# A hybrid decoder layer on one core: the split of the next stage's third weight chunk tied behind the first token block's squares and gain products

## The chip, the cores and the metric

The kernel runs on one core of one Trainium2 chip. The metric is the device time of one execution in microseconds (us), and a kernel's time is the median of its runs. The engines are TensorE (PE in the profile, its weight loads PEld), VectorE (DVE), ScalarE (ACT), GpSimd (POOL) and SyncE (SP, which here only issues loads).

## The reference

One decoder layer over 256 tokens of width 1024 in float32: a SwiGLU block, a mixer (a Mamba-2 branch and a differential attention branch, merged by gates), and a second SwiGLU block. Each stage has a norm in front and one behind:

```python
h = h + 0.5 * rmsnorm(swiglu(rmsnorm(h, ffn1_pre_g[l]), ffn1_w_gate[l], ffn1_w_up[l], ffn1_w_down[l]),
                      ffn1_post_g[l])
u = rmsnorm(h, mix_pre_g[l])
z, xbc, dt_raw, q, k, v, gate_logits = jnp.split(u @ w_in[l], IN_SPLITS, axis=-1)
...
h = h + rmsnorm(merged @ w_out[l], mix_post_g[l])
h = h + 0.5 * rmsnorm(swiglu(rmsnorm(h, ffn2_pre_g[l]), ffn2_w_gate[l], ffn2_w_up[l], ffn2_w_down[l]),
                      ffn2_post_g[l])
```

So there are two turns from one stage to the next: the first SwiGLU into the mixer, and the mixer into the second SwiGLU. At each, a product's result goes through the norm behind the old stage, is added to h, goes through the norm in front of the new stage, and is multiplied by the new stage's first weights.

## The kernel before

**Weights.** All weights are read once, in chunks of 1 MB that are listed in the order of their use. `load_to` issues the load of a chunk on SP into one of three `raw` buffers. A matmul takes a float32 number as two parts: `split_steps` makes, for each half of a chunk, a rounded part `whi` by a cast on ScalarE (L250) and the rest `wlo = raw - whi` by a subtraction on VectorE (L253). Each product is then three matmuls, hi by hi, lo by hi and hi by lo. When all four instructions of a chunk are done its raw buffer is free, and the load of the chunk three further on goes into it. `split_to(n)` splits the chunks up to the n-th, `ahead_of(i, n)` says which chunk lies n ahead of the i-th, and `take` hands out a chunk's parts, splitting some way ahead (`AHEAD` is 3).

**The turn.** The tokens are two blocks of 128. `mm_n` is the last product of a stage, with weights of its own. It keeps the last three chunks (`TAIL`) back and multiplies block 0 with all of them first, its 512-wide left half and then its right half, so that block 0's norm can run while TensorE does block 1. In `mm_n`, `ready(0)` puts block 0's norm into the program, `split_to(ahead_of(taken[0], AHEAD - 1))` the split of the next stage's first two chunks, then come block 1's matmuls (with `turned()` between its halves, which transposes block 0's new h and puts its gain in), `split_to(ahead_of(taken[0], AHEAD))` with the third chunk, and `ready(1)`, block 1's norm.

**The norm behind a stage**, `post_norm`, handles a half at a time. `sum_sq` squares it on ScalarE and sums along the row (L442, `jp_f` or `jp_mxp`). VectorE multiplies the half by the gain (L541, `og`). Behind `mm_quads` the half is first summed from two parts on VectorE (L785: `p_f` and `u_f` for block 0's halves, `u_f` and `c_f` for block 1's). POOL makes the reciprocal root, an add and a power (L447, L448, `rp`), and VectorE updates h (L550). The norm in front of the next stage squares h on ScalarE (`sq_mx`, `sq_f`), and POOL makes `r_mx` or `r_f`. For block 0, the class `Norm` transposes h itself on TensorE (L456, `pu_mx`, `pu_f`) and ScalarE and VectorE make the hi and lo parts with the gain (L462, L464, `u_mx`, `u_f`), the row factor coming later. For block 1, VectorE first multiplies by the factor (L501, `un_mx`, `un_f`), and TensorE transposes that. `products` is the next stage's first products, `pn_mx` and `pn_f` (L335): 12 matmuls for each of four chunks and each block, block 0 first, with block 1's transposes written after the third twelve.

**What sets the order.** From `own_order(PE)` in `mm_n` to the end of `products`, TensorE's instructions run as they are written, and a scheduler that works with estimated times places those of the other engines. An instruction waits for what it reads, and each engine runs its own queue in order.

Of the kernel before, what the change touches and what calls it, by code (L numbers as in the profile page):

```python
# [16 lines left out]
F32 = mybir.dt.float32  # L17
F32R = mybir.dt.float32r
AF = mybir.ActivationFunctionType
ALU = mybir.AluOpType  # L20
# [8 lines left out]
D = 1024  # L29
# [24 lines left out]
def tile_hybrid_layer(ctx: ExitStack, tc: tile.TileContext, x, ffn1_pre_g, ffn1_w_gate, ffn1_w_up,  # L54
# [4 lines left out]
    nc = tc.nc  # L59
# [5 lines left out]
    def k4(shape, name, dt=F32):  # L65
        return sb.tile(shape, dt, tag="k4", name=name, bufs=K4_BUFS)
# [4 lines left out]
    def k2(shape, name, dt=F32):  # L71
        return sb.tile(shape, dt, tag="k2", name=name, bufs=K2_BUFS)

    def jk(shape, name):
        return sb.tile(shape, F32, tag="jk", name=name, bufs=2)

    def tiny(n, name):
        return sb.tile([P, n], F32, tag=f"tiny{n}", name=name, bufs=10)
# [5 lines left out]
    def pjt(name):  # L84

        return pj(name).rearrange("p (m t) -> p m t", m=2)

    def bg(shape, name):
        return ps.tile(shape, F32, tag="bg", name=name, bufs=5)
# [127 lines left out]
    ffn_chunks("f2", ffn2_w_gate, ffn2_w_up, ffn2_w_down)  # L217

    raws, splits = [], []
    taken = [0]  # L220

    def load_to(n):
        while len(raws) < min(n, len(chunks)):
            i = len(raws)
            src, shape = chunks[i]
            r = sb.tile(shape, F32, tag="raw", name=f"raw{i}", bufs=RAW_BUFS)
            nj = shape[1] // 4 if i == 0 else shape[1] // 2 if i < 4 else shape[1]
            for j in range(0, shape[1], nj):
                nc.sync.dma_start(r[:, j:j + nj, :], src[:, j:j + nj, :])
            raws.append(r)  # L230

    def split_steps(ahead=True):


        i, _ = units[len(splits)]
        load_to(i + 1)
        r, shape = raws[i], chunks[i][1]
        nj = shape[1] // 2
        his, los = [], []
        splits.append((his, los))  # L240
        for q in range(2):
            hi = k4([P, nj, shape[2]], f"whi{i}{q}", F32R)
            lo = k4([P, nj, shape[2]], f"wlo{i}{q}", F32R)
            his.append(hi)
            los.append(lo)
            n = 1 if i == 0 else nj
            for j in range(0, nj, n):
                js = slice(j, j + n)
                copy = nc.scalar.copy if i + q + j else nc.vector.tensor_copy
                copy(hi[:, js, :], r[:, q * nj + j:q * nj + j + n, :])  # L250
                if not i + q + j:
                    yield
                nc.vector.tensor_sub(lo[:, js, :], r[:, q * nj + j:q * nj + j + n, :], hi[:, js, :].bitcast(F32))  # L253
                yield
        raws[i] = None
        if ahead:
            load_to(i + 1 + RAW_BUFS)

    def split_to(n):

        while len(splits) < min(n, len(units)):
            of, p = units[len(splits)]
            if p is not None:
                splits.append(of.split(p))
                continue
            for _ in split_steps():
                pass

    def ahead_of(i, n):

        n *= 4
        while n > 0 and i < len(units):
            n -= 4 if units[i][1] is None else 1
            i += 1
        return i

    def take(ahead=AHEAD):

        i = taken[0]
        taken[0] += 1  # L280
        split_to(ahead_of(i, ahead))
        (of, p), w = units[i], splits[i]
        splits[i] = None
        if p is not None:
            return w
        his, los = w
        nj = chunks[of][1][1] // 2
        return (lambda j: his[j // nj][:, j % nj, :], lambda j: los[j // nj][:, j % nj, :])
# [63 lines left out]
    order = mybir.DependencyInfo(mybir.DependencyClass.NoSync, mybir.DependencyReason.DATA)  # L352
# [8 lines left out]
    def act(*args, **kw):  # L361
        a = nc.scalar.activation(*args, **kw)
        if act_fence[0] is not None:
            tc.add_manual_dep(a.ins, act_fence[0], order, reason="activation table")
        act_since.append(a.ins.name)
# [4 lines left out]
    def own_order(*engines):  # L370

        if not ordered[0]:
            order_of[0].enter_context(tc.manual_schedule(engines=set(engines)))
            ordered[0] = True
# [13 lines left out]
    halves = (slice(0, 512), slice(512, D))  # L388
# [32 lines left out]
    for name, v in (("mx", mix_pre_g), ("f2", ffn2_pre_g),  # L421
                    ("ng", ssd_norm_g), ("cb", ssd_conv_b), ("sg", da_subln_g)):
        n = v.shape[1] // P
# [15 lines left out]
    def sum_sq(ss, src, fold, name):  # L439

        junk = jk([P, 512], name)
        nc.scalar.activation(junk, src, AF.Square, scale=(fold / D) ** 0.5, accum_out=ss)  # L442

    def rstd_of(ss, fold, name):

        r = tiny(1, name)
        nc.gpsimd.tensor_scalar(r, ss[:, 0:1], ss[:, 1:2], fold * EPS, ALU.add, ALU.add)  # L447
        f = nc.gpsimd.tensor_tensor(r, r, nhalf, ALU.pow)  # L448
        last_pool[0] = f.ins
        return r  # L450
# [80 lines left out]
    def post_norm(b, acc, pg, fold, tag, last=False):  # L531

        ss = tiny(2, f"sp_{tag}{b}")
        og = []
        for q in range(2):
            sum_sq(ss[:, q:q + 1], acc[q], fold, f"jp_{tag}{b}{q}")
            if last and q == 0:
                e = tiny(1, f"ep_{tag}{b}")
                nc.vector.tensor_scalar(e, ss[:, 0:1], fold * EPS, None, ALU.add)
            og.append(k2([P, 512], f"og_{tag}{b}{q}"))  # L540
            nc.vector.tensor_tensor(og[q], acc[q], pg[:, halves[q]], ALU.mult)  # L541
        if last:
            r = tiny(1, f"rp_{tag}{b}")
            act(r, ss[:, 1:2], AF.Ln, bias=e)
            act(r, r, AF.Exp, scale=-0.5)
        else:
            r = rstd_of(ss, fold, f"rp_{tag}{b}")
        for q in range(2):
            hq = h[:, b, halves[q]]
            nc.vector.scalar_tensor_tensor(hq, og[q], r, hq, ALU.mult, ALU.add)  # L550

    def load_gain(v, name):
        pg = k4([P, D], name)
        nc.gpsimd.dma_start(pg, v[0].partition_broadcast(P))
        return pg

    def mm_n(acc, acts, ready, turned, begun=lambda: None, pairs=None, begin=True, taken_all=lambda: None):

        pairs = pairs or range(len(acts) // 2)
        n = len(pairs)
        held = []

        def one(i, w, parts):
            wh, wl = w
            for kt in range(2):
                ah, al = acts[2 * pairs[i] + kt]
                for b, qs in parts:
                    ts = slice(b * P, (b + 1) * P)  # L570
                    for x_, w_ in ((ah, wh), (al, wh), (ah, wl)):
                        for q in qs:
                            nc.tensor.matmul(acc[b][q], x_[:, ts], w_(kt)[:, halves[q]],  # L573
                                             start=begin and i == 0 and kt == 0 and x_ is ah and w_ is wh,
                                             stop=i == n - 1 and kt == 1 and w_ is wl)
                if i == 0:
                    begun()

        for i in range(n):
            w = take(min(n - i, AHEAD))  # L580
            if i < n - TAIL:
                one(i, w, ((0, (0, 1)), (1, (0, 1))))
            else:
                held.append((i, w))
        taken_all()
        own_order(PE)
        for q in range(2):
            for i, w in held:
                one(i, w, ((0, (q,)),))
        ready(0)  # L590
        split_to(ahead_of(taken[0], AHEAD - 1))
        for q in range(2):
            for i, w in held:
                if q == 1 and i == n - TAIL:
                    turned()
                one(i, w, ((1, (q,)),))
        split_to(ahead_of(taken[0], AHEAD))
        ready(1)

    def sums_of(g, even, odd):  # L600
# [130 lines left out]
    def ffn(post_v, tag, ready, turned, then, products):  # L731
# [51 lines left out]
        def done(b):  # L783
            for q in range(2):
                nc.vector.tensor_tensor(rest[b][q], acc[b][q], rest[b][q], ALU.add)  # L785
            post_norm(b, rest[b], pg, 4.0, tag, ready is store)
            ready(b)

        mm_n(acc, gu, done, turned, pairs=pairs, begin=False,
             taken_all=combine)  # L790

# [16 lines left out]
    raised(1, 0)  # L808
    warm(FILL)
    steps = split_steps(False)  # L810
    next(steps)
    raw(0, 0)
# [75 lines left out]
    norm = made[0]  # L888
# [142 lines left out]
    for i in range(4):  # L1031
        acc = pjt(f"pbc{i}")
# [284 lines left out]
    for g in range(4):  # L1317
        xs[g] = k4([P, 4, T], f"xs{g}")
        for i in range(2):
            acc = pjt(f"pxs{g}{i}")  # L1320
# [5 lines left out]
    for g in range(4):  # L1326
        sz[g] = k4([P, 4, T], f"sz{g}")
        for i in range(2):
            acc = pjt(f"pz{g}{i}")
# [98 lines left out]
    pg = load_gain(mix_post_g, "pg_mx")  # L1428
    acc = [[bg([P, 512], f"acc_mx{b}{q}") for q in range(2)] for b in range(2)]
# [3 lines left out]
    def mixed(b):  # L1433
        post_norm(b, acc[b], pg, 1.0, "mxp")
        ready(b)

    mm_n(acc, mg, mixed, turned, lambda: turn_merged(1))


    norm = made[0]  # L1440
# [36 lines left out]
```

## Time and profile before

| what | value |
|---|---|
| median of 3 runs | 737.97 us (737.88 to 738.38) |
| the profiled execution's own time | 737.54 us |
| span of its records | 735.8 us |
| loads from HBM | 136.17 MB, 187 GB/s over the span |
| the cast L250, 225 of them | 1044 ns mean |
| the subtraction L253, 226 of them | 1208 ns mean |

A row of the timeline is: start in us from the span's start, length in us, engine, line, operation, output and inputs, shapes, count, and in brackets the engine's idle time before it and what ended it. Rows of the same kind are merged, with their count. Instructions of one engine overlap a little, so a step is better read from start to start than from a length. In a view of stretches each row has the stretch, its length, the busy time of TensorE, its weight loads, VectorE, ScalarE and POOL with the number of instructions, the granted TensorE clock as a share of full speed, the busy share of the DMA engines, and GB/s.

### The profile page before, as it was taken

Reading aid. Unit: us, or ns where it says so; the run is one execution under the profiler, and the core shown is the slowest. Engines: PE = TensorE matmul, PEld = TensorE weight load, DVE = VectorE, ACT = ScalarE, POOL = GpSimd, SP = SyncE. Lnnn points to the kernel's source line nnn. Section 1 sums busy time; section 2 is a strip of 40 time slices with the busy share of each in tenths; the row PEclk is TensorE's granted clock in tenths of the full one; section 3 lists DMA queues with packets and bytes.
Section 4 is the critical chain, followed back from the end, with each engine's and each line's share of the span. In section 5 each row is a group of like instructions: output and inputs, shape, how many; then the busy total and the mean of one; then the engine's idle time right before and its main releaser. Section 6 shows DMA issues by size and latency. Waiting matters only on the chain.

```text
span 735.8 us, 10869 instructions
## 1 busy us (share of the span) xinstructions
PE 726.4 (99%) x4211; PEld 628.1 (85%) x4211; DVE 591.9 (80%) x904; ACT 462.1 (63%) x777; POOL 38.6 (5%) x72
## 2 busy tenths in 40 slices
PE   8999999999999999999999999999999999999996
PEld 6888888888889999999888788888888888888874
DVE  7978768998677878787996998785784878779994
ACT  7657556665566565958975577782663657566562
POOL 2700000000300000000000000000010000000000
PEclk9999999999999999999999999999999999999998
DMA  8884674469353647567464664475470765664541
GB/s 299 229 261 150 218 229 171 155 216 348 118 172 117 201 143 226 192 188 226 146 219 154 202 222 138 152 238 191 127 241 34 229 199 153 222 217 143 188 168 57
DMA packets 94212, 137.96 MB, mean 187 GB/s; under 512 B 2684, under 2 KB 68304, under 8 KB 94160
## 3 DMA queue, kind: packets, MB, share of 16 engines
q1 hardware_dynamic: 91488, 129.51, 54.2%
q0 software_dynamic: 2368, 7.22, 3.1%
q8 instruction: 33, 0.54, 0.3%
q10 hardware_dynamic: 304, 0.53, 0.2%
q14 instruction: 19, 0.16, 0.1%
HBM read 136.17 MB, written 1.08 MB: 187 GB/s over the span
## 4 chain that ended last, share of the span: by engine, by line
PE 97%; DVE 2%; issue 1%; DMA 0%; ACT 0%; DVEq 0%
PE pup_f L316 9%; PE pg_f L316 9%; PE pgt L335 6%; PE pws L335 6%; PE acc_f1p L625 5%; PE acc_f2p L625 4%; PE pg_f L315 4%; PE pup_f L315 4%; PE pn_f L335 3%; PE pn_mx L335 3%; PE acc_mx L573 3%; PE pn_f L345 3%; PE pwd L335 3%; PE acc_f1p L573 3%; PE pz L302 2%; PE pxs L304 2%
## 5 line engine op out<-in xcount | busy, mean ns | idle before, releaser
L253 DVE TENSOR_TENSOR wlo<-raw,whi 128x1024 fp32r<-128x1024 f32 (+1 forms) x226 | 266.6, 1208 | 22.7 <-ACT whi L250 21.7
L250 ACT CAST whi<-raw 128x1024 fp32r<-128x1024 f32 (+1 forms) x225 | 226.2, 1044 | 18.1 <-DMA raw<-in_w_in_dram 3.8
L316 PE MATMUL pup_f<-u_f,whi 128*128 128x512 f32 x288 | 101.3, 396 | 0.0
L316 PE MATMUL pg_f<-u_f,whi 128*128 128x512 f32 x288 | 101.2, 396 | 0.0
L315 PE MATMUL pg_f<-u_f,wlo 128*128 128x256 f32 x252 | 70.6, 280 | 0.0
L315 PE MATMUL pup_f<-u_f,wlo 128*128 128x256 f32 x252 | 70.3, 279 | 0.0
L316 PEld LDWEIGHTS pup_f<-u_f,whi 128*128 128x128 f32 x288 | 52.8, 188 | 9.8
L316 PEld LDWEIGHTS pg_f<-u_f,whi 128*128 128x128 f32 x288 | 52.8, 188 | 9.6
L315 PEld LDWEIGHTS pg_f<-u_f,wlo 128*128 128x128 f32 x252 | 47.5, 188 | 1.7
L315 PEld LDWEIGHTS pup_f<-u_f,wlo 128*128 128x128 f32 x252 | 47.5, 189 | 1.6
L321 DVE TENSOR_TENSOR su_f<-pup_f,su_f 128x256 f32<-128x256 f32 x36 | 15.1, 420 | 26.0 <-ACT su_f L320 25.8
L130 ACT CAST wqh<-wt 128x1024 fp32r<-128x1024 f32 x20 | 21.0, 1052 | 23.2 <-DVE wt L122 23.2
L320 ACT COPY su_f<-pup_f 128x256 f32<-128x256 f32 x36 | 13.4, 373 | 35.1 <-PE pup_f L316 34.9
L335 PE MATMUL pgt<-whi,u_mx 128*128 128x512 f32 x128 | 33.1, 393 | 0.0
L301 PE MATMUL pxs<-u_mx,whi 128*128 128x256 f32 x128 | 31.7, 285 | 0.0
L302 PE MATMUL pz<-u_mx,whi 128*128 128x256 f32 x128 | 31.6, 284 | 0.0
L301 PE MATMUL pz<-u_mx,whi 128*128 128x256 f32 x128 | 31.6, 284 | 0.0
L302 PE MATMUL pxs<-u_mx,whi 128*128 128x256 f32 x128 | 31.4, 283 | 0.0
L335 PEld LDWEIGHTS pgt<-whi,u_mx 128*128 128x128 f32 x128 | 23.6, 188 | 5.4 <-issue 0.7
L1009 DVE SCALAR_TENSOR_TENSOR xs<-pxs,cols_b,xs 128x255 f32<-128x255 f32 (+2 forms) x48 | 21.9, 475 | 6.3 <-ACT xs L1006 5.9
L291 ACT CAST gh_f<-sg_f 128x512 fp32r<-128x512 f32 x18 | 11.2, 622 | 21.5 <-DVE sg_f L771 21.5
L302 PEld LDWEIGHTS pz<-u_mx,whi 128*128 128x128 f32 x128 | 24.5, 192 | 0.2 <-issue 0.2
(397 smaller groups left out, 1698.5 us busy)
## 6 DMA issues: line engine op xcount, KB each, us to landing
raw<-in_w_in_dram SPq DMA_DIRECT2D x40, 1024.0 KB, 5.4
raw<-in_ffn_w_down_dram SPq DMA_DIRECT2D x22, 1024.0 KB, 4.9
raw<-in_ffn_w_gate_dram SPq DMA_DIRECT2D x20, 1024.0 KB, 5.6
raw<-in_ffn_w_up_dram SPq DMA_DIRECT2D x20, 1024.0 KB, 5.4
raw<-in_ssd_w_branch_dram SPq DMA_DIRECT2D x8, 1024.0 KB, 5.3
acb<-acd POOLq DMA_DIRECT2D x8, 512.0 KB, 5.5
raw<-in_da_w_branch_dram SPq DMA_DIRECT2D x4, 1024.0 KB, 5.1
raw<-in_w_out_dram SPq DMA_DIRECT2D x4, 1024.0 KB, 5.0
```

Source lines behind the costliest of these rows:

```text
L130: nc.scalar.copy(hi, src)
L250: copy(hi[:, js, :], r[:, q * nj + j:q * nj + j + n, :])
L253: nc.vector.tensor_sub(lo[:, js, :], r[:, q * nj + j:q * nj + j + n, :], hi[:, js, :].bitcast(F32))
L301: nc.tensor.matmul(acc[m], wh(j)[:, cs], ah(k0 + j), start=first and j == ks[0], stop=False)
L302: nc.tensor.matmul(acc[m], wh(j)[:, cs], al(k0 + j), start=False, stop=False)
L315: nc.tensor.matmul(acc[:, :T], wl(j)[:, cs], ah(j), start=False, stop=False)
L316: nc.tensor.matmul(acc, wh(j)[:, cs], ahl(j), start=j == 0, stop=j == KD - 1)
L335: nc.tensor.matmul(acc, a(k0 + j), b(j), start=first and i == 0, stop=last and i == 11)
L345: nc.tensor.matmul(accs[b], x_(k0 + j), w_(j), start=first and j == 0 and w_ is wh and x_ is acts[b][0], stop=last and j == 3 and w_ is wl)
L573: nc.tensor.matmul(acc[b][q], x_[:, ts], w_(kt)[:, halves[q]], start=begin and i == 0 and kt == 0 and x_ is ah and w_ is wh, stop=i == n - ...
L625: nc.tensor.matmul(bank[p], x_, w_, start=p not in begun, stop=last and p in (1, 5, 6, 7))
L1009: nc.vector.scalar_tensor_tensor(dst[:, m, s:], acc[:, m, :T - s], cw(3 - s, c), dst[:, m, s:], ALU.mult, ALU.add)
```

## The change

At each turn the program remembers two instructions of block 0's norm: the last square sum (of the right half, `norm_sq`) and the last gain product (of the right half, `last_og`). While the third chunk of the next stage is being split, each of its casts gets an edge behind that square and each of its subtractions an edge behind that product. The edges set the order alone (`NoSync`): they add no semaphore. The computation is the same.

```diff
     raws, splits = [], []
+    lo_fence, last_og, last_sq, norm_sq = [], [None], [None], [None]
     taken = [0]
...
                 copy = nc.scalar.copy if i + q + j else nc.vector.tensor_copy
-                copy(hi[:, js, :], r[:, q * nj + j:q * nj + j + n, :])
+                m = copy(hi[:, js, :], r[:, q * nj + j:q * nj + j + n, :])
+                if lo_fence:
+                    tc.add_manual_dep(m.ins, lo_fence[1].name, order, reason="behind a norm's squares")
                 if not i + q + j:
                     yield
-                nc.vector.tensor_sub(lo[:, js, :], r[:, q * nj + j:q * nj + j + n, :], hi[:, js, :].bitcast(F32))
+                m = nc.vector.tensor_sub(lo[:, js, :], r[:, q * nj + j:q * nj + j + n, :], hi[:, js, :].bitcast(F32))
+                if lo_fence:
+                    tc.add_manual_dep(m.ins, lo_fence[0].name, order, reason="behind a norm's products")
                 yield
...
     def sum_sq(ss, src, fold, name):
...
-        nc.scalar.activation(junk, src, AF.Square, scale=(fold / D) ** 0.5, accum_out=ss)
+        last_sq[0] = nc.scalar.activation(junk, src, AF.Square, scale=(fold / D) ** 0.5, accum_out=ss).ins
...
     def post_norm(b, acc, pg, fold, tag, last=False):
...
             sum_sq(ss[:, q:q + 1], acc[q], fold, f"jp_{tag}{b}{q}")
+            norm_sq[0] = last_sq[0]
...
-            nc.vector.tensor_tensor(og[q], acc[q], pg[:, halves[q]], ALU.mult)
+            last_og[0] = nc.vector.tensor_tensor(og[q], acc[q], pg[:, halves[q]], ALU.mult).ins
...
         ready(0)
+        of0 = last_og[0], norm_sq[0]
         split_to(ahead_of(taken[0], AHEAD - 1))
...
+
+        lo_fence.extend(of0)
         split_to(ahead_of(taken[0], AHEAD))
+        lo_fence.clear()
         ready(1)
```

At the end of the second SwiGLU, `mm_n` runs once more with no chunk left to split, and nothing is tied there. The scheduler places the other engines' instructions anew. In the order that results, VectorE and ScalarE differ from before at the two turns alone; TensorE, POOL and SP keep theirs. On VectorE at the first turn, the third chunk's two subtractions come after both updates of h instead of before block 0's two `og`, and block 1's first `og` comes after the `u_mx` instead of before them. At the second turn they come after both updates of h as well. On ScalarE one cast of the third chunk comes ahead of and one between the two squares of h (`sq_mx`, `sq_f`), instead of ahead of block 0's squares (at the second turn, between them).

## The prediction

> **What bounds the kernel now.** I read the page's busy times first, then its chain of work that ended last, then the engines' busy time in stretches cut where the change acts.
>
> ```profile
> PE 726.4 (99%) x4211; PEld 628.1 (85%) x4211; DVE 591.9 (80%) x904; ACT 462.1 (63%) x777; POOL 38.6 (5%) x72
> PE 97%; DVE 2%; issue 1%; DMA 0%; ACT 0%; DVEq 0%
> 180.00:204.00 24.00, 24.00 (x116) 19.91 (x115) 16.64 (x34) 12.99 (x37) 6.44 (x10) 1.00 0.46 143
> 204.00:538.00 334.00, 333.98 (x2197) 296.23 (x2196) 273.30 (x454) 222.47 (x390) 6.42 (x12) 1.00 0.58 184
> 538.00:557.00 19.00, 19.00 (x94) 15.89 (x93) 11.87 (x21) 10.41 (x29) 4.69 (x9) 1.00 0.54 177
> 557.00:716.00 159.00, 159.00 (x836) 135.24 (x834) 132.64 (x174) 97.62 (x141) 0.63 (x1) 1.00 0.54 176
> ```
>
> TensorE bounds it. In the last four rows the first number is the stretch's length and the second TensorE's busy time, and they agree: 24.00 of 24.00 us around the first stage turn, 19.00 of 19.00 around the second, and what follows each is as full (333.98 of 334, 159.00 of 159). Two things follow. There is no gap of TensorE at either turn that an earlier square or product could close, so the gain there is nothing, or what overlapping matmul records can hide, some tenths. And no gap after 204 us can take up a stall, so whatever TensorE waits there is paid in full.
>
> **The first turn now.** TensorE, from its timeline:
>
> ```profile
> 181.50 0.39 PE L573 MATMUL acc_f1p<-wlo,gh_f 128*128 128x512 f32 x1
> 185.81 1.03 PE L456 MATMUL pu_mx<-ident,h 128*128 128x128 f32 x8
> 190.82 1.17 PE L335 MATMUL pn_mx<-whi,u_mx 128*128 128x512 f32 x4
> 198.21 1.07 PE L335 MATMUL pn_mx<-whi,u_mx 128*128 128x512 f32 x4
> 199.03 0.88 PEld L456 LDWEIGHTS pu_mx<-ident,un_mx 128*128 128x128 f32 x8 [0.18 <-DVE un_mx L501]
> 199.12 1.04 PE L456 MATMUL pu_mx<-ident,un_mx 128*128 128x128 f32 x8
> ```
>
> Block 0's second half of the down product ends at 181.50 + 0.39 = 181.89, its transposes stand at 185.81, the next stage's products begin at 190.82, and block 1's transposes sit between them at 199.12. From 190.82 to 198.21 lie 32 matmuls, 0.231 us each, so after four more the transposes are due at 199.13. They began on time, but their weight load had already waited 0.18 us for un_mx. Block 1's norm is thus just in time, with under 0.1 us to spare.
>
> VectorE at the same turn:
>
> ```profile
> 180.85 1.22 DVE L253 TENSOR_TENSOR wlo<-raw,whi 128x1024 fp32r<-128x1024 f32 x1
> 181.99 0.68 DVE L785 TENSOR_TENSOR u_f<-acc_f1p,u_f 128x512 f32<-128x512 f32 x1
> 184.60 1.41 DVE L550 SCALAR_TENSOR_TENSOR h<-og_f,rp_f,h 128x512 f32<-128x512 f32 x2 [1.21 <-POOL rp_f L448]
> 186.01 0.69 DVE L785 TENSOR_TENSOR u_f<-acc_f1p,u_f 128x512 f32<-128x512 f32 x1
> 186.73 0.69 DVE L541 TENSOR_TENSOR og_f<-u_f,pg_f 128x512 f32<-128x512 f32 x1
> 187.89 2.16 DVE L464 SCALAR_TENSOR_TENSOR u_mx<-pu_mx,cols_a,u_mx 128x128 fp32r<-128x128 f32 x8 [0.47 <-ACT u_mx L462]
> 190.48 1.23 DVE L253 TENSOR_TENSOR wlo<-raw,whi 128x1024 fp32r<-128x1024 f32 x1 [0.42 <-ACT whi L250]
> 191.62 0.68 DVE L785 TENSOR_TENSOR c_f<-acc_f1p,c_f 128x512 f32<-128x512 f32 x1
> 193.00 1.22 DVE L253 TENSOR_TENSOR wlo<-raw,whi 128x1024 fp32r<-128x1024 f32 x1
> 195.07 1.41 DVE L550 SCALAR_TENSOR_TENSOR h<-og_f,rp_f,h 128x512 f32<-128x512 f32 x2 [0.85 <-POOL rp_f L448]
> 198.38 1.02 DVE L501 TENSOR_SCALAR un_mx<-h,r_mx 128x512 f32<-128x512 f32 x2 [1.90 <-POOL r_mx L448]
> ```
>
> **What the move gains: nothing.** The lo at 180.85, the second of the third chunk, is what now runs ahead of block 0's sum u_f, and it ends its turn at 181.99. TensorE itself releases u_f only at 181.89, so without the lo the norm starts at most 0.1 us earlier; I take 0.05. The transposes at 185.81 follow TensorE's own last matmul anyway.
>
> **What the move costs at the first turn.** The instruction order of the changed program differs from the old one only at the two turns, and only on VectorE and ScalarE. TensorE, POOL and the loads keep their order. On VectorE both lo parts of the third chunk now stand behind the two h updates, and block 1's first product og_f (186.73) moves behind the eight u_mx. Queued behind the lo parts are u_f (186.01), u_mx, the fourth chunk's first lo (190.48) and c_f (191.62), block 1's last sum. Everything from c_f on is block 1's norm, which TensorE waits for. On ScalarE the two casts now stand one ahead of and one between the squares of h:
>
> ```profile
> 185.44 0.63 ACT L442 ACTIVATE sq_mx<-h 128x512 f32<-128x512 f32 x1 [2.02 <-DVE h L550]
> 186.11 0.63 ACT L442 ACTIVATE sq_mx<-h 128x512 f32<-128x512 f32 x1
> 186.74 2.16 ACT L462 ACTIVATE u_mx<-pu_mx,cols_a 128x128 fp32r<-128x128 f32 x8
> 188.74 0.67 ACT L442 ACTIVATE jp_f<-u_f 128x512 f32<-128x512 f32 x1
> 189.35 2.04 ACT L250 CAST whi<-raw 128x1024 fp32r<-128x1024 f32 x2
> ```
>
> ScalarE first. The first cast fits into the 2.02 us that ScalarE idles before its square. Two casts take 2.04 us, so the second, between the squares, pushes the rest by about 0.95. The squares start 0.67 apart: square at 185.40, cast at 186.07, second square at 187.02, u_mx at 187.65 instead of 186.74. That is 0.91 later.
>
> VectorE next, a lo costing 191.62 - 190.48 = 1.14. The h pair starts at 184.55 and frees the engine 1.32 later, at 185.87. The first lo runs then. The second needs its cast (186.07 + 1.05, and 0.06 to pass it on) and starts at 187.18, and u_f at 188.32. The u_mx start at 188.92; their condition from ScalarE is 187.65 + 1.15 = 188.80 (1.15 is 187.89 - 186.74 now), met by 0.12. Eight of them take 2.08, og_f starts at 191.00, the fourth chunk's lo at 191.60 (its cast is ready at about 191.4), and c_f at 192.74 instead of 191.62: 1.12 later. So of 2 x 1.14 = 2.28 us inserted, about half falls into idle time that stood there (the 0.47 and 0.42 in the rows, and some waiting before u_f and og_f), and 1.1 remains.
>
> From c_f to un_mx each step waits for the one before, so 1.1 carries through:
>
> ```profile
> 193.22 1.17 POOL L447 TENSOR_SCALAR rp_f<-sp_f 128x1 f32<-128x1 f32 x1 [4.98 <-ACT jp_f L442]
> 194.47 0.56 POOL L448 TENSOR_TENSOR rp_f<-rp_f,nhalf 128x1 f32<-128x1 f32 x1
> 197.40 0.30 POOL L447 TENSOR_SCALAR r_mx<-ss_mx 128x1 f32<-128x1 f32 x1 [2.36 <-ACT sq_mx L442]
> ```
>
> The add on POOL takes 1.17 here and 0.30 where VectorE is idle. The fourth chunk's second lo runs from 193.00 to 194.22 and the add ends 0.17 after it. In the changed order the lo still starts before the add, at 194.12, so I keep 1.17. Were the add to take 0.30, the chain would be 0.87 shorter and only some 0.2 us would be left.
>
> The Trainium skill (SBUF — State Buffer, section Who interferes with whom) says that a VectorE instruction with two SBUF inputs and a GpSimd instruction that reads SBUF exclude each other for a whole instruction. By that rule the add ends with the lo wherever both move, and the stall stays at 1.05; the rows at 193.00 and 193.22 agree with it.
>
> TensorE's transposes then start at about 199.12 + 1.1 less the 0.05 to 0.1 to spare: **a stall of 1.05 us**. Bounds: 0 if the lo parts were swallowed entirely, and 2 x 1.14 less the spare, 2.2, if no idle time took any; I take 1.05, as the rows place each step.
>
> **What stays covered there.** ScalarE's u_mx end by 189.8 instead of 188.9, ahead of the products at 190.82. The third chunk's weights are ready at 188.4, while TensorE reaches it after 24 matmuls, at 196.4. Its raw buffer goes back 6.2 us later, which delays one load of the SP queue:
>
> ```profile
> 182.09 12.52 SPq L229 DMA_DIRECT2D raw<-in_w_in_dram  x2
> raw<-in_w_in_dram SPq DMA_DIRECT2D x40, 1024.0 KB, 5.4
> 203.52 2.93 ACT L250 CAST whi<-raw 128x1024 fp32r<-128x1024 f32 x3
> ```
>
> Issued at 188.3 instead of 182.09, it lands 5.4 later, at 193.7. The third cast at 203.52, at about 205.4, is its first reader, 11.7 us behind. Without that cover every us of lateness would reach the cast. The load behind it on SP, issued at 194.2, moves with the stall only.
>
> **The second turn.** The same edit, with the norm's inputs read straight from PSUM:
>
> ```profile
> 541.41 0.63 ACT L442 ACTIVATE sq_f<-h 128x512 f32<-128x512 f32 x1 [2.10 <-DVE h L550]
> 543.35 2.17 ACT L462 ACTIVATE u_f<-pu_f,cols_a 128x128 fp32r<-128x128 f32 x8
> 543.48 0.69 DVE L541 TENSOR_TENSOR og_mxp<-acc_mx,pg_mx 128x512 f32<-128x512 f32 x1 [1.50 <-ACT jp_mxp L442]
> 547.48 1.07 PE L335 MATMUL pn_f<-whi,u_f 128*128 128x512 f32 x4
> 553.11 1.02 DVE L501 TENSOR_SCALAR un_f<-h,r_f 128x512 f32<-128x512 f32 x2 [1.90 <-POOL r_f L448]
> 555.65 1.04 PE L456 MATMUL pu_f<-ident,un_f 128*128 128x128 f32 x8
> ```
>
> The lo parts go into the 1.50 us idle before og_mxp, and what remains is ScalarE's cast between the squares, again 0.95: og_mxp at about 544.4, un_f at 553.7 to 554.3. At the first turn the transposes began 0.74 after un_mx (199.12 - 198.38), so here un_f may start as late as 555.65 - 0.74 = 554.91, 1.8 later than now. A shift of 0.6 to 1.2 is hidden by that. The u_f of ScalarE end at 546.5, ahead of the products at 547.48. Cost 0; without the 1.8 it would be the whole shift.
>
> **The sum.** Span 735.80 + 1.05 + 0 = 736.85; the profiled execution took 737.54, 1.74 more than its span, so 738.59. It lies 0.43 under the median 737.97, and the forecast in the median's terms is 739.0. No change can be told within 0.2%, 1.48 us: 736.5 to 739.45. So this is slower by 0.14%, inside that band.
>
> **The rivals.**
> - ScalarE sets the pace (slower). The u_mx of VectorE have only 0.12 us over ScalarE. If cast, square and u_mx in turn take more than the gaps read above, the idle 0.47 and 0.42 come back and each further tenth is paid. It decides once block 1's c_f is 1.55 late or more. At the limit of 2.2 the time is 740.2; the middle of 1.5 to 2.2 gives 739.8. For it: the thin margin. Against it: each gap is one that the same instructions show now. Chance 0.20.
> - Hidden after all, stall under 0.4: the add on POOL gets ahead of the lo and ends in 0.30, or the lo parts overlap better. 737.97 + 0.2 = 738.2. Against it: jp_f follows c_f by longer than the lo does. 0.11.
> - Faster, from a stall hidden in overlapping records at the turns: 24.00 of 24.00 us speaks against it, and beyond 1.48 us it would need more than 6% of that stretch. 736.4. 0.03.
> - The order changes nothing because the edges carry no wait: excluded by the changed instruction order, where the lo parts do stand behind h.
>
> **How the numbers follow.** Forecast 0.66, rivals 0.20, 0.11, 0.03. Forecast and hidden case lie mostly within the band: 0.76 after moving 0.01 to slower for the forecast's upper tail. Slower 0.21, faster 0.03. The range 737.9 to 740.3 goes from no stall to no idle time taken, with 0.1 for the scatter of the runs.
>
> **What would show it.** Right: the weight load of block 1's transposes, ahead of pn_mx's fourth chunk, with an idle of about 1.2 put to un_mx, TensorE idle for about 1 us near 199, c_f near 192.7, u_f (block 0's sum) still near 181.95. The second turn's un_f near 554 with TensorE full. Wrong: c_f earlier than 192.2, a 0.3 us add in front of block 1's h, an idle of TensorE at 555, or a cast waiting for raw near 205.

## The result, and the profile after

The changed kernel takes 738.96 us (median of 22 runs, 738.51 to 741.45), the kernel before 737.98 us (22 runs, 737.45 to 739.4). The ratio is 1.0014, 95% interval 1.0007 to 1.0020: slower by 1.0 us. The profiled execution took 738.63 us with a span of 736.9, against 735.8 before.

The page after, busy times and chain of work that ended last:

```profile
PE 727.2 (99%) x4211; PEld 629.1 (85%) x4211; DVE 592.2 (80%) x904; ACT 461.5 (63%) x777; POOL 39.4 (5%) x72
PE 93%; DVE 4%; issue 1%; ACT 1%; POOL 0%; DMA 0%; DVEq 0%; ACTq 0%; POOLq 0%
```

The work is the same, the chain is not: it leaves TensorE for VectorE, ScalarE and POOL for a stretch. The stretches of both turns show which:

```profile
180.00:204.00 24.00, 23.22 (x111) 19.06 (x110) 16.58 (x34) 13.45 (x37) 6.48 (x10) 1.00 0.46 144
539.10:558.10 19.00, 19.00 (x94) 15.90 (x93) 12.59 (x21) 11.89 (x31) 5.37 (x9) 1.00 0.55 177
558.10:717.10 159.00, 158.97 (x836) 135.12 (x834) 132.73 (x174) 97.51 (x141) 0.63 (x1) 1.00 0.53 176
```

TensorE now lacks 0.78 of the 24 us around the first turn, nothing around the second, and 0.03 of the 159 us behind it. TensorE and its weight loads there:

```profile
190.87 1.17 PE L340 MATMUL pn_mx<-whi,u_mx 128*128 128x512 f32 x4
198.26 1.07 PE L340 MATMUL pn_mx<-whi,u_mx 128*128 128x512 f32 x4
200.10 0.86 PEld L461 LDWEIGHTS pu_mx<-ident,un_mx 128*128 128x128 f32 x8 [1.20 <-DVE un_mx L506]
200.10 1.09 PE L461 MATMUL pu_mx<-ident,un_mx 128*128 128x128 f32 x8 [0.78 <-DVE un_mx L506]
200.95 1.17 PE L340 MATMUL pn_mx<-whi,u_mx 128*128 128x512 f32 x4
```

The products begin within 0.05 us of when they did (190.87, before 190.82). Block 1's transposes wait for un_mx. The idle shown, 0.78, is less than the delay because the end of a matmul is modelled in the profile and overlaps what follows: from the start of the products to the first product behind the transposes are 10.08 us (200.95 - 190.87), before 9.09 (199.91 - 190.82). The stall is 0.99 us.

VectorE in front of it:

```profile
181.98 0.69 DVE L795 TENSOR_TENSOR u_f<-acc_f1p,u_f 128x512 f32<-128x512 f32 x1 [1.93 <-PE acc_f1p L579]
184.60 1.42 DVE L556 SCALAR_TENSOR_TENSOR h<-og_f,rp_f,h 128x512 f32<-128x512 f32 x2 [1.21 <-POOL rp_f L453]
185.94 2.44 DVE L256 TENSOR_TENSOR wlo<-raw,whi 128x1024 fp32r<-128x1024 f32 x2
188.29 0.68 DVE L795 TENSOR_TENSOR u_f<-acc_f1p,u_f 128x512 f32<-128x512 f32 x1
188.89 2.15 DVE L469 SCALAR_TENSOR_TENSOR u_mx<-pu_mx,cols_a,u_mx 128x128 fp32r<-128x128 f32 x8
191.56 1.22 DVE L256 TENSOR_TENSOR wlo<-raw,whi 128x1024 fp32r<-128x1024 f32 x1
192.69 0.68 DVE L795 TENSOR_TENSOR c_f<-acc_f1p,c_f 128x512 f32<-128x512 f32 x1
194.08 1.22 DVE L256 TENSOR_TENSOR wlo<-raw,whi 128x1024 fp32r<-128x1024 f32 x1
196.14 1.42 DVE L556 SCALAR_TENSOR_TENSOR h<-og_f,rp_f,h 128x512 f32<-128x512 f32 x2 [0.85 <-POOL rp_f L453]
199.45 1.02 DVE L506 TENSOR_SCALAR un_mx<-h,r_mx 128x512 f32<-128x512 f32 x2 [1.89 <-POOL r_mx L453]
```

The two moved lo parts are the row at 185.94. Above them nothing is earlier: u_f starts at 181.98 (181.99 before), now after 1.93 us of idle, and h at 184.60 in both. Below them everything is later, c_f by 1.07 and un_mx by 1.07. The idle times of 0.47 and 0.42 before are gone. TensorE's work runs 0.05 us later in this trace than in the one before, so against TensorE u_f and h come 0.05 to 0.06 earlier, and c_f and un_mx 1.02 later.

The chain of work that ended last, in order of time around this turn, goes through just these rows (start, length, engine, tile; lines between them are left out). In the kernel before, the same view has TensorE alone.

```profile
186.02 2.36 DVE wlo L256 x2
188.38 0.60 DVE u_f L795
191.64 1.13 DVE wlo L256
192.78 0.61 DVE c_f L795
194.30 1.18 POOL rp_f L452
199.45 0.61 DVE un_mx L506
200.10 1.09 PE pu_mx L461 x8
```

### The profile page after: what moved, and what is told of

It reads as the page before. It is cut to its first block, busy times and chain, and to the rows that moved or that the text cites. A ratio compares the mean times of both kernels' runs of the same rounds, so it can differ in the third digit from the quotient of the medians.

```text
span 736.9 us, 10868 instructions
## 1 busy us (share of the span) xinstructions
PE 727.2 (99%) x4211; PEld 629.1 (85%) x4211; DVE 592.2 (80%) x904; ACT 461.5 (63%) x777; POOL 39.4 (5%) x72
## 4 chain that ended last, share of the span: by engine, by line
PE 93%; DVE 4%; issue 1%; ACT 1%; POOL 0%; DMA 0%; DVEq 0%; ACTq 0%; POOLq 0%
PE pup_f L321 9%; PE pg_f L321 9%; PE pws L340 6%; PE pgt L340 6%; PE acc_f1p L635 5%; PE pg_f L320 4%; PE pup_f L320 4%; PE pn_f L350 3%; PE pn_f L340 3%; PE acc_mx L579 3%; PE pwd L340 3%; PE acc_f2p L635 2%; PE pz L307 2%; PE pxs L309 2%; PE pz L309 2%; PE pxs L307 2%
## 5 line engine op out<-in xcount | busy, mean ns | idle before, releaser
L135 DVE TENSOR_TENSOR wql<-wt,wqh 128x1024 fp32r<-128x1024 f32 x20 | 24.4, 1221 | 0.2
```

Of the source, the lines that this page charges most:

```text
L135: last_lo[0] = nc.vector.tensor_sub(lo, src, hi.bitcast(F32)).ins
```

## The experiments

The theory: the stall comes from the two lo parts that stand ahead of block 1's last sum on VectorE at the first turn, and POOL's add is tied to the lo that runs beside it. The rivals: the second turn pays a part, the casts on ScalarE or the late loads cost, or the add is long for a reason of its own.

Executions differ by up to 2.1 us in their first 30 us, and a stall of 0.2 us is less than that. So the stalls are read within a trace: from the first `pg_f` matmul, the first work behind the opening products, to the first product behind block 1's transposes at each turn, less the same in the kernel before (199.91 - 30.43 and 556.45 - 30.43). The last column has what was added up to the first turn's mark and up to the second's. The stretch behind the second mark varies too, from 179.35 us in the kernel before to 179.78 in the kernel with the first turn only, which was not followed up. Spans of single executions therefore miss the expected ones by some tenths even where the stall came as expected: 736.3 instead of 735.8 (second turn only), 736.7 instead of 736.15 (changed, fourth lo late), 736.1 instead of 735.7 to 735.8 (before, fourth lo late).

| kernel | ratio to before, 95% | first `pg_f` | first turn | second turn | added by each mark |
|---|---|---|---|---|---|
| changed | 1.0014 (1.0007 to 1.0020) | 30.48 | 200.95 | 557.46 | 0.99, 0.96 |
| first turn only | 1.0014 (1.0005 to 1.0024) | 32.53 | 203.00 | 559.52 | 0.99, 0.97 |
| second turn only | 0.9997 (0.9988 to 1.0006) | 30.68 | 200.18 | 556.72 | 0.02, 0.02 |
| lo edges only | 1.0012 (1.0003 to 1.0021) | 30.48 | 200.75 | 557.30 | 0.79, 0.80 |
| changed, fourth lo late | 1.0008 (0.9999 to 1.0017) | 30.84 | 200.52 | 557.07 | 0.20, 0.21 |
| before, fourth lo late | 0.9996 (0.9986 to 1.0007) | 30.73 | 200.22 | 556.74 | 0.01, -0.01 |
| before, second turn pushed | 1.0011 (1.0003 to 1.0020) | 30.83 | 200.32 | 557.41 | 0.01, 0.56 |
| lo parts behind block 1 | 1.0021 (1.0011 to 1.0030) | 32.52 | 202.65 | 560.14 | 0.65, 1.60 |

**One turn at a time.** `mm_n` gets `pairs` only from the SwiGLU stages, so that tells the turns apart:

```diff
+        of_ffn = pairs is not None
...
-        lo_fence.extend(of0)
+        if of_ffn:                      # the other kernel: if not of_ffn
+            lo_fence.extend(of0)
```

> The edges at the first turn alone. Theory (the two lo parts in front of block 1's last sum c_f at the first turn make the stall, the second turn costs nothing): as the changed kernel, c_f near 192.7, block 1's transposes at 200.1 with an idle of about 0.8 on TensorE, span 736.9, ratio to before 1.0014. Rival (the second turn pays a part): shorter than the changed kernel by that part. Rival (the late raw buffers and loads cost): the same share at each turn, so about 736.3.

> The edges at the second turn alone. Theory: no stall; un_f about 0.6 later than before against TensorE (near 553.7) and still over 1 us ahead of its transposes at 555.65, span 735.8, ratio 1.0000. Rival (the second turn pays a part): span over 736.1 with an idle of TensorE near 555.

Measured: the first turn alone gives the ratio of the whole change and the same 0.99 us; the second turn alone gives none. In the first, c_f stands 1.82 behind the start of the products (194.75 - 192.93), as in the changed kernel (192.69 - 190.87). The span there was 739.3 and not 736.9: that execution lost 2.05 us before 33 us, and some 0.3 between the second turn and the end. In the second, un_f started at 554.01, which is 0.65 later than before once the late start of 0.25 is taken off, and the transposes came on time. The rival of the second turn falls. So does that of the late loads: in the second kernel the load at the second turn was issued 4.5 us later than before (544.47 - 0.25 against 539.72) and cost nothing, and in the changed kernel the casts behind the first turn did not wait for a load.

**Only the edges of the lo parts.** The edges of the lo parts stay, those of the casts are left out. The opposite, the edges of the casts alone, was not run.

```diff
-                if lo_fence:
-                    tc.add_manual_dep(m.ins, lo_fence[1].name, order, reason="behind a norm's squares")
```

> The edges of the casts are left out, those of the lo parts stay. The scheduler then puts the third chunk's first lo at the first turn in front of the h updates, where VectorE waits 1.2 us for POOL, and the second behind them. Theory with the exclusion of POOL's add by a VectorE instruction with two SBUF inputs: the add at 183.6 takes about 1.1 instead of 0.31 and ends 0.17 after the lo, h starts near 185.4 instead of 184.6, block 0's transposes stall TensorE by about 0.6 near 186, block 1's by 0.1 to 0.3 near 200, span 736.4 to 736.7. Rival (no exclusion: the add's 1.17 at block 1 has another cause): the first lo is free in that gap, h stays at 184.6, c_f at about 191.6, span 735.8.

Its POOL and VectorE rows at the first turn, and TensorE's weight loads for the transposes of blocks 0 and 1:

```profile
183.31 1.22 DVE L254 TENSOR_TENSOR wlo<-raw,whi 128x1024 fp32r<-128x1024 f32 x1
183.60 1.11 POOL L450 TENSOR_SCALAR rp_f<-sp_f 128x1 f32<-128x1 f32 x1 [20.02 <-ACT jp_f L445]
185.40 1.41 DVE L554 SCALAR_TENSOR_TENSOR h<-og_f,rp_f,h 128x512 f32<-128x512 f32 x2 [0.87 <-POOL rp_f L451]
186.21 0.42 PEld L459 LDWEIGHTS pu_mx<-ident,h 128*128 128x128 f32 x4 [0.61 <-DVE h L554]
186.87 0.42 PEld L459 LDWEIGHTS pu_mx<-ident,h 128*128 128x128 f32 x4 [0.24 <-DVE h L554]
199.90 0.86 PEld L459 LDWEIGHTS pu_mx<-ident,un_mx 128*128 128x128 f32 x8 [0.37 <-DVE un_mx L504]
```

The lo in VectorE's idle gap is not free. It runs to 184.53, and POOL's add, 0.31 in the changed kernel, takes 1.11 and ends 0.18 after it. h comes 0.8 later, and the products 0.64 (191.51 - 30.48 against 190.82 - 30.43). Block 1's transposes add 0.15, together 0.79. Theory and place are as expected, the span of 736.8 is 0.1 above the upper end of what was expected. The rival without exclusion falls.

This run also shows what one lo costs in front of c_f. With one between h and c_f, and no cast between block 0's squares, c_f starts 7.10 behind h (192.50 - 185.40). It was 7.02 in the kernel before and is 8.09 with two in the changed kernel. So the idle time there takes up nearly all of one lo, and the second is paid.

The Trainium skill (SBUF — State Buffer, section Who interferes with whom) says that a VectorE instruction with two SBUF inputs contends with a GpSimd instruction that reads SBUF, and that one with at most one SBUF input, outside the two-port performance modes, does not. The trace agrees on both: above the lo has two, and at the second turn of the changed kernel the add ran in 0.31 beside og_mxp, which reads PSUM and SBUF.

```profile
540.36 0.69 DVE L547 TENSOR_TENSOR og_mxp<-acc_mx,pg_mx 128x512 f32<-128x512 f32 x1 [2.43 <-ACT jp_mxp L447]
540.42 0.31 POOL L452 TENSOR_SCALAR rp_mxp<-sp_mxp 128x1 f32<-128x1 f32 x1 [31.76 <-ACT jp_mxp L447]
```

The nine traces have 72 such adds at the two turns. The 37 that started while VectorE ran a lo or an og_f with both inputs in SBUF each ended 0.15 to 0.18 behind it, whatever was left of it, and took 0.38 to 1.17. The other 35, eight of them beside og_mxp, took 0.30 or 0.31.

**The fourth chunk's second lo behind block 1's h**, in the changed kernel and in the one before:

```diff
-            ws = [take(1) for _ in range(4)]
+            ws = [take(1) for _ in range(3)]
+            late4[0] = True
+            ws.append(take(1))
+            late4[0] = False
...
                 m = nc.vector.tensor_sub(lo[:, js, :], r[:, q * nj + j:q * nj + j + n, :], hi[:, js, :].bitcast(F32))
+                if late4[0] and q:
+                    tc.add_manual_dep(m.ins, last_h[0].name, order, reason="behind block 1's h")
```

`last_h` is the last h update that `post_norm` made.

> The changed kernel, with the fourth chunk's second lo tied behind block 1's h update at both turns. Theory with the exclusion: POOL's add of block 1 at 194.3 takes 0.3 instead of 1.17, h starts near 195.3 instead of 196.1, the lo then follows h and un_mx starts near 198.7 instead of 199.45; the stall shrinks to about 0.35, span 736.15, ratio 1.0005. Rival (the add takes 1.17 for a reason of its own): h and un_mx stay, span 736.9.

> The kernel before, with the fourth chunk's second lo tied behind block 1's h update at both turns. Theory (TensorE has no gap at the turns, so an earlier norm gains nothing): un_mx 0.7 to 0.9 earlier than 198.38, the weight load's wait of 0.18 gone, transposes still at 199.1, span 735.7 to 735.8, ratio 1.000. Rival (block 1's norm already costs TensorE something that the overlapping records hide): span shorter by more than 0.15.

The add, h, the lo behind it, un_mx and the weight load of the transposes in the first kernel (0.36 of later start in its times):

```profile
194.64 0.30 POOL L455 TENSOR_SCALAR rp_f<-sp_f 128x1 f32<-128x1 f32 x1 [5.10 <-ACT jp_f L450]
195.62 1.41 DVE L559 SCALAR_TENSOR_TENSOR h<-og_f,rp_f,h 128x512 f32<-128x512 f32 x2 [1.11 <-POOL rp_f L456]
196.95 1.22 DVE L257 TENSOR_TENSOR wlo<-raw,whi 128x1024 fp32r<-128x1024 f32 x1
199.02 1.02 DVE L509 TENSOR_SCALAR un_mx<-h,r_mx 128x512 f32<-128x512 f32 x2 [0.85 <-POOL r_mx L456]
199.67 0.86 PEld L464 LDWEIGHTS pu_mx<-ident,un_mx 128*128 128x128 f32 x8 [0.41 <-DVE un_mx L509]
```

With no lo beside it the add takes 0.30, h and un_mx come earlier, and of the stall 0.20 is left, less than the 0.35 expected. So the rival, an add that is long for a reason of its own, falls. The transposes follow un_mx by 0.65 (199.67 - 199.02), as in the changed kernel (200.10 - 199.45); the 0.74 read off the kernel before held 0.1 of spare time. In the kernel before, the same edge brought un_mx 0.83 forward and TensorE nothing:

```profile
197.85 1.02 DVE L504 TENSOR_SCALAR un_mx<-h,r_mx 128x512 f32<-128x512 f32 x2 [0.84 <-POOL r_mx L451]
199.20 1.02 PEld L459 LDWEIGHTS pu_mx<-ident,un_mx 128*128 128x128 f32 x8
199.42 1.04 PE L459 MATMUL pu_mx<-ident,un_mx 128*128 128x128 f32 x8
```

The weight load's wait is gone, the transposes start 0.91 behind the matmuls ahead of them as they always did, and the ratio is 0.9996 with 1 inside its interval. An earlier norm has nothing to gain at this turn.

**How much the second turn takes.**

```diff
             self.un = [unit(1, q, r, self.tag, nc.vector) for q in range(2)]
+            for _ in range(3 if self.tag == "f2" else 0):
+                for q in range(2):
+                    nc.vector.tensor_scalar(self.un[q], h[:, 1, halves[q]], r, None, ALU.mult)
```

> The kernel before, with both halves of un_f written three times more at the second turn (the same values). Theory (the second turn is free only within its 1.8 us of spare time): the last passes of un_f start 3.0 to 3.6 later, near 556.4, and TensorE's transposes wait 1.2 to 1.8 past 555.65, span 737.0 to 737.6. Rival (the second turn takes up any such delay, for instance since other work of TensorE could go first): span 735.8.

```profile
553.51 1.02 DVE L501 TENSOR_SCALAR un_f<-h,r_f 128x512 f32<-128x512 f32 x2 [1.90 <-POOL r_f L448]
554.46 2.45 DVE L689 TENSOR_SCALAR un_f<-h,r_f 128x512 f32<-128x512 f32 x6
556.57 0.86 PEld L456 LDWEIGHTS pu_f<-ident,un_f 128*128 128x128 f32 x8 [0.80 <-DVE un_f L689]
556.57 1.09 PE L456 MATMUL pu_f<-ident,un_f 128*128 128x128 f32 x8 [0.38 <-DVE un_f L689]
```

The added passes stand only 0.40 apart (2.45 for six, each 0.47), so the last pass over the left half starts at about 556.04, 2.5 later than the first and not 3.0 to 3.6. Less the spare time of 1.9 (555.65 - 0.65 - 553.11) that is 0.6, and 0.56 was measured. The rival falls: beyond its spare time the second turn pays in full. The size expected was wrong, because the passes follow each other faster than the 0.5 to 0.6 that it was worked out from.

**The lo parts behind block 1's norm.** The third chunk's casts keep their edge, its lo parts come into the program after `ready(1)`:

```diff
-                m = nc.vector.tensor_sub(lo[:, js, :], ...)
-                if lo_fence:
-                    tc.add_manual_dep(m.ins, lo_fence[0].name, order, ...)
+                if lo_fence:
+                    after.append(lambda ...: nc.vector.tensor_sub(...))
...
         ready(1)
+        for f in after:
+            m = f()
+            if m is not None:
+                tc.add_manual_dep(m.ins, last_og[0].name, order, reason="behind block 1's products")
```

> The casts as in the changed kernel, but the third chunk's lo parts put into the program behind block 1's norm and tied behind its last gain product. On VectorE nothing of the third chunk is then left between h and c_f. Theory: c_f starts at its own release by TensorE, near 191.0, 1.7 earlier than in the changed kernel; but lo parts now stand beside POOL's add and ahead of un_mx, and the exclusion lets un_mx gain little: un_mx 198.2 to 199.0, stall 0 to 0.6, span 735.8 to 736.4. Rival (casts between h and the squares on ScalarE make the stall): as the changed kernel or worse, 736.9, with c_f late.

Its times are 2.09 late from the start:

```profile
193.08 0.69 DVE L805 TENSOR_TENSOR c_f<-acc_f1p,c_f 128x512 f32<-128x512 f32 x1 [0.98 <-PE acc_f1p L584]
197.38 0.64 ACT L452 ACTIVATE sq_mx<-h 128x512 f32<-128x512 f32 x1 [2.79 <-DVE h L561]
198.01 1.03 ACT L251 CAST whi<-raw 128x1024 fp32r<-128x1024 f32 x1
198.95 0.63 ACT L452 ACTIVATE sq_mx<-h 128x512 f32<-128x512 f32 x1
199.76 0.71 POOL L457 TENSOR_SCALAR r_mx<-ss_mx 128x1 f32<-128x1 f32 x1 [3.27 <-ACT sq_mx L452]
201.15 1.02 DVE L511 TENSOR_SCALAR un_mx<-h,r_mx 128x512 f32<-128x512 f32 x2 [0.85 <-POOL r_mx L458]
557.85 0.73 PE L345 MATMUL pn_f<-wlo,u_f 128*128 128x512 f32 x2 [0.66 <-DVE wlo L258]
```

c_f now starts where TensorE releases it, at 190.99. From block 1's h (196.53) to un_mx (201.15) are 4.62 us, 1.31 more than in the changed kernel (199.45 - 196.14), and un_mx starts at 199.06, just over the expected 199.0. The lo parts made the smaller part of that: the second add on POOL takes 0.71 instead of 0.30, beside a lo. The larger part is on ScalarE and was not expected. The scheduler put a cast of the fourth chunk between block 1's two squares, which now stand 1.57 apart (0.66 in the changed kernel), and the add starts 0.91 later for it. So the start of un_mx came close to the forecast for a reason that is only in part the one given. The stall of 0.65 is 0.05 above the range. The second miss is larger: at the second turn the scheduler put lo parts behind un_f, TensorE waited for one of them, and 0.95 more was lost there. The rival on the casts wanted c_f late, which it is not. But the scheduler put both casts of the third chunk ahead of block 0's squares here, so this run does not clear the cast that stands between them in the changed kernel. That it costs nothing by itself was not tried; in the changed kernel the `u_mx` of VectorE start 0.60 after u_f with no idle time, so ScalarE was not what held them, and its cast held up the second lo by 0.07 at most (187.15 instead of 185.94 + 1.14).

No version beat the kernel before.

## Why the prediction was right

**What bounds the kernel, and the gain of nothing.** Right. The first turn has no gap to close: block 0's u_f and h start within 0.01 us of where they did, which against TensorE is the 0.05 earlier that was forecast, and an un_mx 0.83 earlier gained nothing in the kernel before.

**The cost on VectorE and ScalarE.** Each start came as worked out: the squares at 185.45 and 187.02 with the cast at 186.08 between (185.40, 187.02, 186.07), u_mx on ScalarE at 187.64 (187.65) and on VectorE at 188.89 (188.92), c_f at 192.69 (192.74). The margin of 0.12 over ScalarE held, so the rival in which ScalarE sets the pace did not come. That rival was close: the margin measured is 0.10 (188.89 less 187.64 + 1.15).

**The chain through POOL.** Right. The add took 1.17 again, beside the lo at 194.08, and un_mx moved by the same 1.07 as c_f. The rival in which the add gets ahead of the lo did not come by itself; with the lo moved out of the add's way, it is worth 0.8 of the stall. One reading was loose there: the row of jp_f starts ahead of the lo, and not behind it. The add waits for the read of jp_f's sum, which ends 0.12 behind the lo's start in both kernels (193.12 against 193.00, and 194.20 against 194.08).

**The size.** 0.99 us instead of 1.05. Against TensorE un_mx came 1.02 later. Of that the spare time in front of the transposes took 0.09, near the upper end of the bracket, so they started 0.93 late. Another 0.06 came behind that, since from their start to the next product are 0.85 instead of 0.79. The span was forecast at 736.85 and is 736.9, the time at 739.0 and is 738.96. That the times agree to 0.04 is in part luck, since the interval of the ratio reaches from 0.5 to 1.5 us; the stall read within the trace is the better test. The band of 0.2% in which no change was thought to show was too wide: with 22 runs of each kernel the interval leaves out 1.

**The covers.** The third chunk's raw buffer went back later, its load was issued at 188.41 (188.3 in the forecast), and the casts from 204.57 on did not wait for a load. The second turn's un_f came 0.65 later against TensorE, within 0.6 to 1.2, and found 1.9 of spare time; pushed past it, the turn pays.

## What to carry to other kernels

On an engine that runs its queue in order, a piece of work that is moved out of one chain's way stands in the way of the next. Its price is its length less the idle time it finds in the new place, and its gain is bounded by what the bottleneck engine waited for in the old one; here that was nothing. Compare the start of an instruction with the end of what releases it before clearing its way: u_f was held by TensorE, and by the lo ahead of it for 0.06 us at most. Idle time of VectorE beside a POOL step is not free for an instruction with two SBUF inputs, since it can hold up that step, here for 0.8 us. And after tying one kind of instruction, read the order of the others too: with the lo parts moved away, a cast of another chunk landed between two squares and delayed what follows by 0.91.

## What the runs showed that was not expected

The opening of the kernel scatters more than the change is worth: the first `pg_f` matmul came between 30.43 and 32.53 us over these traces. In the trace with 32.53, the eight first products that need 2.93 us in the changed kernel's trace took 3.76, after TensorE had waited 0.60 for a part of x. In the one with 32.52 they took 3.74, after a wait of 0.87 for a cast. What slowed them was not followed up. A difference of 0.1% in this kernel is read from stretches within a trace, or from many runs.
